# Eighteen instead of nine seven-product tiles in a feed-forward on one Trainium2 core

## The chip, the core and the metric

The kernel runs on one core of a Trainium2 chip. The core has a matrix engine (TensorE, PE in the profile; its weight loads are listed as PEld), a vector engine (VectorE, DVE), an activation engine (ScalarE, ACT), a general engine (GpSimd, POOL) and a queue engine that issues DMAs (SyncE, SP). The time is device microseconds of one execution. Three timed runs of the kernel before gave 1910.76, 1911.52 and 1913.13 us.

## What is computed

Four blocks work on one sequence of 512 tokens with 1024 features, all in float32: a recurrent layer with pooling (`even`), an attention over keys chosen by an index (`odd`), a sliding-window attention with a feed-forward (`swa`, `ffn`), and an attention over compressed, chosen and near keys with a second feed-forward (`nsa`, `ffn`). The parts that the change touches are these:

```python
def rms_norm(x, g):
    y = x32 * lax.rsqrt(jnp.mean(x32 * x32, axis=-1, keepdims=True) + RMS_EPS)
    return y * g
def swiglu(h, w_gu, w_down):                      # D_FF = 2816 = 22 tiles of 128
    gate, up = jnp.split(h @ w_gu, 2, axis=-1)
    return (jax.nn.silu(gate) * up) @ w_down
# second_block, both layers: h = h + swiglu(rms_norm(h, ffn_norm[layer]), ffn_w_gu[layer], ffn_w_down[layer])
# odd_layer: the attention's output is multiplied by silu(z), z a slice of xn @ w_in
```

## The kernel before

Features lie on the 128 partitions and the 512 tokens along the free axis, so the residual is eight tiles X[k] of 128x512. A product keeps float32 accuracy by splitting both factors into a rounded part and a rest (`h` and `l`, type fp32r) and issuing three matmuls: high by high, high by low, low by high (`mm3`, lines 152 to 154). A weight tile is loaded by SP into a `raw` buffer; for each 512 columns ScalarE rounds it into `wh` (line 133) and VectorE or GpSimd takes the rest into `wl` (line 134). The list `wpool["l"]` says which of the two takes the rests of a plain weight. In the feed-forward there are 4 raw buffers and 10 pairs of `wh`, `wl`.

The norm is not multiplied into the matmuls' input: `n.xh`, `n.xl` hold x times the gain, and what a product gives is multiplied by the broadcast reciprocal root `n.RB` afterwards.

In `ffn` a hidden tile j (128 of the 2816 features) needs a gate product and an up product, each with a contraction over 8 feature tiles. A *dense* tile does both plainly: 2 x 8 x 3 = 48 matmuls of 512 columns (`pg`, `pu`). A *scheme* tile (`scheme`, lines 1460 to 1497) treats gate and up as a 2x2 block product over even and odd feature tiles and over the two halves of the tokens, and does it with seven half-size products: 7 x 4 x 3 = 84 matmuls of 256 columns (`pw`). For it, `scheme_weights` forms seven combinations of the raw weights (`s1`, `s2`, differences written back into `raw`), rounds each and takes its rest (lines 1443 and 1444); `token_sums` forms the matching combinations of the tokens once (`ta`, `tb`, split into `th`, `tl`); and eight small operations (lines 1489 to 1496) add the seven products up into `g` and `u`. Before the change, tiles 5, 7, ..., 21 are scheme tiles and the other 13 are dense. Then `g` and `u` give the hidden value: a tanh on ScalarE, two operations on VectorE (1516, 1517) and a split into `hh`, `hl`. The down product (`dn`) is taken over tiles 0 to 7, 8 to 15 and 16 to 21, each time with eight steps of 8 or 6 contraction tiles, between the hidden tiles.

In `ffn` the order on each engine is chosen when the program is built; in `odd` and `nsa` TensorE's order is written by hand: a `Filler` holds a list of projection items, and `f.fill(n)` issues the next n pieces of them between the pieces of the attention. In `odd`, a search for the 256 best keys runs on VectorE (`rounds`: MAX and MATCH_REPLACE, lines 901 and 902) and ends in a `mask` that the attention logits need. A gate projection `zgate` is multiplied by RB (line 826) and turned into silu (lines 1048 and 1049) when its product is done. In `nsa`, `blocks` arranges compressed keys and values into `zp` and splits them (`zh`, `zl`).

Of the kernel before, what the change touches and what calls it, by code (L numbers as in the profile page):

```python
# [31 lines left out]
def kernel(ctx: ExitStack, tc: tile.TileContext, a: dict, out: bass.AP, upto: int = 9, start: int = 1):  # L32
# [783 lines left out]
    def odd(n):  # L816
# [227 lines left out]
        def zgate(m):  # L1044
            def done(ps):
                z = evac(ps)
                t = th[m] = lp.tile([P, T], F32, tag="th", name="th", bufs=6)
                act.activation(t, z, AF.Tanh, scale=0.5)
                dve.scalar_tensor_tensor(t, t, 1.0, z, op0=ALU.add, op1=ALU.mult)
            return proj(5 + m, done)  # L1050

# [19 lines left out]
        with tc.manual_schedule(engines={pe.engine}):  # L1071
# [10 lines left out]
            def k_t(g, j):  # L1082
                return to_feature("kt", kT, g, gqk, j)

            f = Filler([proj(3, index_query), proj(0, latent), proj(1, latent), queries(0), keys(0), zgate(0),
# [5 lines left out]
                        mid(values(3), {2: q_t(3, 0)}), mid(out_part(1, 0), {3: k_t(3, 0), 7: k_t(3, 1)}),  # L1091
                        mid(zgate(6), {1: q_t(3, 1)}), out_part(1, 1), zgate(7),
# [9 lines left out]
            f.fill(9)  # L1102
            index_weights()
            top = topk(1)
# [9 lines left out]
            for i in (2, 3):  # L1114
                for h in range(4):
                    score(i, h)
                    f.fill(1)
                    rounds(1)
            f.fill(3)
            latent_stat()  # L1120
            for i in range(13):
                f.fill(1)
                rounds(1)
                if i == 2:
                    latent_norm()
# [20 lines left out]
            for s in range(len(units) + 3):  # L1146
# [17 lines left out]
                if s >= 3:  # L1164
                    u = s - 3
                    g, j, half, r = units[u]
                    if r == 0:
                        po[g, j, half] = ps_at("po", "po")
                    attend_values(po[g, j, half][:, None, 256 * r:256 * r + 256], half,
# [232 lines left out]
    def ffn(n, layer, gname, goff, after):  # L1402
        es, lp, tmp = open_layer(f"f{layer}", 2, 6, 6, dict(mm=6, at=2))
# [6 lines left out]
        sums = []  # L1410

        def token_sums(q):

            xe, xo, ta, tb = (tmp(nm) for nm in ("xe", "xo", "ta", "tb"))
            for x, k in ((xe, 2 * q), (xo, 2 * q + 1)):
                act.activation(x, X[k], AF.Identity, scale=V("ffn_norm", KD * layer + k))
            t1, t2, t3, t4 = ta[:, :HT], ta[:, HT:], tb[:, :HT], tb[:, HT:]
# [10 lines left out]
        def scheme_weights(j):  # L1428
# [19 lines left out]
            part(a11, dve)  # L1448
# [50 lines left out]
        def hidden(j):  # L1499
            if j >= 5 and j % 2:  # L1500
                g, u = scheme(j)
                pool.tensor_mul(g, g, n.RB)
                dve.tensor_mul(u, u, n.RB)
            else:
                if j == 6:
                    wpool["l"] = [dve, pool]
# [4 lines left out]
                dve.tensor_mul(u, pu, n.RB)  # L1511
            if j < 4:
                token_sums(j)
            th = tmp("th")
            act.activation(th, g, AF.Tanh, scale=0.5)
            dve.scalar_tensor_tensor(th, th, 1.0, g, op0=ALU.add, op1=ALU.mult)
# [635 lines left out]
```

## Time and profile before

| what | value |
|---|---|
| timed runs, median | 1911.52 us |
| profiled execution, its own time | 1910.72 us |
| its span in the trace | 1909.0 us |
| TensorE busy | 1868.6 us (98%), 10334 matmuls |
| VectorE busy | 1360.1 us (71%) |
| ScalarE busy | 1005.0 us (53%) |
| GpSimd busy | 863.8 us (45%) |
| granted TensorE clock, mean | 0.995 |

Matmuls overlap in the pipeline, so a matmul's own duration is longer than its share of the time; what one costs is the distance from its start to the next one's start. Busy time of an engine is read by stage: the two feed-forwards lie at about 900 to 1262 us and 1540 to 1900 us, `odd` at about 480 to 760 us, `nsa` from about 1265 us.

### The profile page before, as it was taken

Reading aid. Unit: us, or ns where it says so; the run is one execution under the profiler, and the core shown is the slowest. Engines: PE = TensorE matmul, PEld = TensorE weight load, DVE = VectorE, ACT = ScalarE, POOL = GpSimd, SP = SyncE. Lnnn points to the kernel's source line nnn. Section 1 sums busy time; section 2 is a strip of 40 time slices with the busy share of each in tenths; the row PEclk is TensorE's granted clock in tenths of the full one; section 3 lists DMA queues with packets and bytes.
Section 4 is the critical chain, followed back from the end, with each engine's and each line's share of the span. In section 5 each row is a group of like instructions: output and inputs, shape, how many; then the busy total and the mean of one; then the engine's idle time right before and its main releaser. Section 6 shows DMA issues by size and latency. Waiting matters only on the chain.

```text
span 1909.0 us, 29335 instructions
## 1 busy us (share of the span) xinstructions
PE 1868.6 (98%) x10334; PEld 1603.1 (84%) x10334; DVE 1360.1 (71%) x2666; ACT 1005.0 (53%) x2079; POOL 863.8 (45%) x842
## 2 busy tenths in 40 slices
PE   8999999999998999999999999999999999999998
PEld 7888888887788888888888898888888888888887
DVE  6776767566698777797786584657999678747553
ACT  6543343434447786696543342347898555324333
POOL 1101001114467575897554453356666455545433
PEclk9999999999999999999999999999999999999999
DMA  4233342322345553411424233333111142423421
GB/s 163 86 109 114 110 144 78 100 78 78 89 127 153 146 158 94 144 45 45 133 89 124 79 107 88 89 131 122 54 45 50 34 144 78 124 76 96 126 75 59
DMA packets 72700, 190.06 MB, mean 100 GB/s; under 512 B 9253, under 2 KB 24101, under 8 KB 72553
## 3 DMA queue, kind: packets, MB, share of 16 engines
q1 hardware_dynamic: 68824, 184.43, 31.8%
q10 hardware_dynamic: 3728, 3.75, 0.6%
q8 instruction: 82, 1.34, 0.3%
q14 instruction: 66, 0.53, 0.1%
HBM read 167.03 MB, written 12.59 MB: 94 GB/s over the span
## 4 chain that ended last, share of the span: by engine, by line
PE 85%; DVE 8%; ACT 2%; DMA 1%; POOL 1%; issue 1%; SPq 0%; DVEq 0%; POOLq 0%; ACTq 0%
PE pj L152 7%; PE pj L153 6%; PE pj L154 6%; PE dn L153 4%; PE dn L152 4%; PE dn L154 4%; PE wo L152 4%; PE wo L154 4%; PE wo L153 4%; PE pw L1484 3%; PE pw L1483 3%; PE pw L1482 3%; PE pu L154 3%; PE pu L153 3%; PE pu L152 3%; PE pg L152 3%
## 5 line engine op out<-in xcount | busy, mean ns | idle before, releaser
L133 ACT CAST wh<-raw 128x512 fp32r<-128x512 f32 (+1 forms) x510 | 306.5, 609 | 396.4 <-PE pj L153 120.8
L134 POOL TENSOR_TENSOR wl<-raw,wh 128x512 fp32r<-128x512 f32 (+1 forms) x226 | 303.5, 1346 | 247.6 <-ACT wh L133 225.1
L134 DVE TENSOR_TENSOR wl<-raw,wh 128x512 fp32r<-128x512 f32 (+1 forms) x284 | 222.1, 788 | 109.8 <-ACT wh L133 103.9
L152 PE MATMUL pj<-xh,wh 128*128 128x512 f32 (+1 forms) x648 | 265.3, 410 | 0.0
L154 PE MATMUL pj<-xh,wl 128*128 128x512 f32 (+1 forms) x648 | 255.4, 394 | 1.0 <-POOL wl L134 0.6
L153 PE MATMUL pj<-xl,wh 128*128 128x512 f32 (+1 forms) x648 | 255.3, 394 | 1.0 <-DVE xl L281 1.0
L154 PEld LDWEIGHTS pj<-xh,wl 128*128 128x128 f32 (+1 forms) x648 | 121.6, 188 | 29.3 <-POOL wl L134 1.0
L153 PEld LDWEIGHTS pj<-xl,wh 128*128 128x128 f32 (+1 forms) x648 | 122.2, 189 | 24.0 <-DVE xl L281 2.1
L153 PE MATMUL dn<-hl,wh 128*128 128x512 f32 (+1 forms) x376 | 141.8, 377 | 0.0
L154 PE MATMUL dn<-hh,wl 128*128 128x512 f32 (+1 forms) x376 | 141.1, 375 | 0.0
L152 PE MATMUL dn<-hh,wh 128*128 128x512 f32 (+1 forms) x376 | 140.7, 377 | 0.0
L152 PEld LDWEIGHTS pj<-xh,wh 128*128 128x128 f32 (+1 forms) x648 | 122.3, 189 | 21.7 <-ACT wh L133 0.9
L152 PE MATMUL wo<-yh,wh 128*128 128x512 f32 x320 | 130.2, 408 | 2.3 <-DVE vv L114 1.4
L153 PE MATMUL wo<-yl,wh 128*128 128x512 f32 x320 | 125.6, 394 | 0.0
L154 PE MATMUL wo<-yh,wl 128*128 128x512 f32 x320 | 125.5, 394 | 0.0
L1444 POOL TENSOR_TENSOR wl<-raw,wh 128x512 fp32r<-128x512 f32 x54 | 76.1, 1410 | 103.5 <-ACT wh L1443 92.4
L744 ACT ACTIVATE L<-L,sm 128x128 f32<-128x128 f32 (+1 forms) x192 | 107.4, 561 | 18.9 <-DVE sm L742 17.8
L742 DVE CUSTOM_DVE_ANT_0 L<-lg,stp 128x128 f32<-128x128 f32 (+1 forms) x192 | 87.6, 482 | 6.3 <-PE lg L796 2.8
L114 DVE TENSOR_TENSOR pl<-pt,ph 128x384 fp32r<-128x384 f32 (+1 forms) x144 | 83.3, 592 | 10.6 <-ACT ph L113 9.3
L1443 ACT CAST wh<-raw 128x512 fp32r<-128x512 f32 x90 | 55.3, 618 | 64.7 <-PE dn L153 33.7
L580 POOL TENSOR_TENSOR up<-u 128x527 f32<-128x527 f32 x8 | 11.1, 1387 | 170.1 <-DVE nq L535 79.5
L323 DVE TENSOR_TENSOR x<-wo,x 128x512 f32<-128x512 f32 x88 | 60.2, 686 | 34.3 <-PE wo L154 33.8
(454 smaller groups left out, 5489.7 us busy)
## 6 DMA issues: line engine op xcount, KB each, us to landing
raw<-in_w_gu SPq DMA_DIRECT2D x88, 512.0 KB, 3.7
raw<-in_w_even SPq DMA_DIRECT2D x48, 512.0 KB, 3.7
raw<-in_w_dn SPq DMA_DIRECT2D x32, 512.0 KB, 3.7
rsc<-rv SPq DMA_DIRECT2D x64, 160.0 KB, 3.8
raw<-in_w_eout SPq DMA_DIRECT2D x16, 512.0 KB, 3.7
stp<-rsc SPq DMA_DIRECT2D x32, 256.0 KB, 3.2
raw<-in_w_odd SPq DMA_DIRECT2D x13, 512.0 KB, 3.8
raw<-in_w_dn SPq DMA_DIRECT2D x16, 384.0 KB, 3.2
```

The lines of the kernel that those rows point to most:

```text
L114: (eng or dve).tensor_sub(l, src, f32(h))
L133: act.copy(h[:, :m], raw[:, o:o + m])
L134: eng[i % len(eng)].tensor_sub(l[:, :m], raw[:, o:o + m], f32(h[:, :m]))
L152: pe.matmul(ps, wh, xh, start=first, stop=False)
L153: pe.matmul(ps, wh, xl, start=False, stop=False)
L154: pe.matmul(ps, wl, xh, start=False, stop=last)
L323: dve.tensor_add(X[k], ps, X[k])
L742: dve.tensor_tensor_reduce(L, lg, strip[:, (1 - ii) * P:], 1.0, -NEG, op0=ALU.add, op1=ALU.min, accum_out=sm[:, ii:ii + 1])
L744: act.activation(L, L, AF.Exp, scale=-1.0, bias=sm[:, ii:ii + 1], accum_out=sm[:, 2 + ii:3 + ii])
L1444: eng.tensor_sub(lv, src, f32(hv))
L1482: pe.matmul(d, h[:, c], xh, start=y == q == 0, stop=False)
L1483: pe.matmul(d, h[:, c], xl, start=False, stop=False)
```

## The change

Tiles 4 to 21 become scheme tiles, 18 of 22. So that they need no multiplication by RB afterwards, the tokens are normed before they are summed: `token_sums` multiplies each x tile by RB on GpSimd, and once the four dense tiles and the down steps over them are issued, `n.xh` and `n.xl` are written anew from the normed tiles. The buffers for that are borrowed from the hidden tiles (12 instead of 11 pairs). The down product is now over tiles 0 to 3, 4 to 9, 10 to 15 and 16 to 21, and the steps of the two middle ones are issued one or two behind each tile from 10 on. In `odd`, `zgate` only copies its product out; norm and silu of it (`silu2`) come when the attention is there. The fills, the index weights and two key transposes of `odd` move by a few pieces. In `nsa` GpSimd takes the weights' rests at first and every second split of `zp`.

```diff
         def zgate(m):
             def done(ps):
-                z = evac(ps)
                 t = th[m] = lp.tile([P, T], F32, tag="th", name="th", bufs=6)
-                act.activation(t, z, AF.Tanh, scale=0.5)
-                dve.scalar_tensor_tensor(t, t, 1.0, z, op0=ALU.add, op1=ALU.mult)
+                with soon():
+                    act.copy(t, ps)
             return proj(5 + m, done)
+        def silu2(m):
+            z, t = th[m], tmp("tz")
+            pool.tensor_mul(z, z, n.RB)
+            act.activation(t, z, AF.Tanh, scale=0.5)
+            dve.scalar_tensor_tensor(z, t, 1.0, z, op0=ALU.add, op1=ALU.mult)
...
-            f = Filler([proj(3, index_query), proj(0, latent), proj(1, latent), queries(0), keys(0), zgate(0),
+            f = Filler([proj(3, index_query), proj(0, latent), proj(1, latent), queries(0), zgate(0), keys(0),
...
-                        mid(values(3), {2: q_t(3, 0)}), mid(out_part(1, 0), {3: k_t(3, 0), 7: k_t(3, 1)}),
-                        mid(zgate(6), {1: q_t(3, 1)}), out_part(1, 1), zgate(7),
+                        mid(values(3), {2: q_t(3, 0)}), mid(out_part(1, 0), {4: k_t(3, 0)}),
+                        mid(zgate(6), {1: q_t(3, 1), 5: k_t(3, 1)}), out_part(1, 1), zgate(7),
...
-            f.fill(9)
+            f.fill(5)
             index_weights()
+            f.fill(4)
...
+            latent_stat()
             f.fill(3)
-            latent_stat()
             for i in range(13):
                 f.fill(1)
                 rounds(1)
-                if i == 2:
+                if i == 1:
                     latent_norm()
...
                         po[g, j, half] = ps_at("po", "po")
+                        if half:
+                            silu2(2 * g + j)
...
     def ffn(n, layer, gname, goff, after):
-        es, lp, tmp = open_layer(f"f{layer}", 2, 6, 6, dict(mm=6, at=2))
+        es, lp, tmp = open_layer(f"f{layer}", 2, 6, 4, dict(mm=6, at=2))
...
         def token_sums(q):
-            xe, xo, ta, tb = (tmp(nm) for nm in ("xe", "xo", "ta", "tb"))
+            xe, xo = (f32(t) for t in hidden_tiles())
+            ta, tb = (f32(t) for t in hidden_tiles())
             for x, k in ((xe, 2 * q), (xo, 2 * q + 1)):
                 act.activation(x, X[k], AF.Identity, scale=V("ffn_norm", KD * layer + k))
+                pool.tensor_mul(x, x, n.RB)
+                normed.append(x)
...
             pool.tensor_add(s1, a21, a22)
-            part(a11, dve)
+            part(a11, pool)
...
         def hidden(j):
-            if j >= 5 and j % 2:
+            if j >= 4:
                 g, u = scheme(j)
-                pool.tensor_mul(g, g, n.RB)
-                dve.tensor_mul(u, u, n.RB)
             else:
-                if j == 6:
-                    wpool["l"] = [dve, pool]
...
-        for j in range(10):
+        for j in range(4):
             hidden(j)
-        down(0, 8, False)
-        for j in range(10, 18):
+        steps = down(0, 4, False)
+        for k in range(KD):
+            run_step(steps)
+            split(n.xh[k], n.xl[k], normed[k])
+        for j in range(4, 22):
+            wpool["l"] = [pool, dve] if j % 2 else [dve, pool]
             hidden(j)
-        down(8, 16, False)
-        for j in range(18, 22):
-            hidden(j)
+            for _ in range(1 + (j % 3 == 0) if j > 9 else 0):
+                run_step(steps)
+            if j in (9, 15):
+                steps = down(j - 5, j + 1, False)
...
-        es, lp, tmp = open_layer("l4", 0, 1, 5, dict(mm=1, at=3, lg=2, po=2), weng=[dve, pool])
+        es, lp, tmp = open_layer("l4", 0, 1, 5, dict(mm=1, at=3, lg=2, po=2), weng=[pool])
...
-                    split(rv[:, :, 0], rv[:, :, 1], zt.rearrange("p (u c) -> p u c", u=4))
+                    split(rv[:, :, 0], rv[:, :, 1], zt.rearrange("p (u c) -> p u c", u=4), pool if t else dve)
...
+            wpool["l"] = [dve, pool]
             f.fill(33)
```

Three places show what moves. The first is VectorE in the first feed-forward, where before a dense tile (`pg`, `pu`) is followed by scheme tile 9 (`pw`; `s_10913` and `s_10914` are its weight sums):

```order
L1510 TENSOR_TENSOR g<-pg,RB 128x512
L134 TENSOR_TENSOR wl<-raw,wh 128x512
L1450 TENSOR_TENSOR s_10914<-s_10913,raw 128x512
L1511 TENSOR_TENSOR u<-pu,RB 128x512
L134 TENSOR_TENSOR wl<-raw,wh 128x512
L1516 SCALAR_TENSOR_TENSOR th<-th,g 128x512
L1517 SCALAR_TENSOR_TENSOR u<-th,u 128x512
L1444 TENSOR_TENSOR wl<-raw,wh 128x512
L1490 TENSOR_TENSOR g<-pw,u 128x256
L114 TENSOR_TENSOR hl<-u,hh 128x512
```

There now one scheme tile follows another; these are the rows from the hidden split of one tile to the second hidden operation of the next:

```order
L114 TENSOR_TENSOR hl<-u,hh 128x512
L1507 TENSOR_TENSOR u<-pw,u 128x256
L1460 TENSOR_TENSOR wl<-raw,wh 128x512
L1508 TENSOR_TENSOR g<-pw,u 128x256
L1509 TENSOR_TENSOR u<-pw,u 128x256
L1510 TENSOR_TENSOR u<-pw,g 128x256
L1511 TENSOR_TENSOR u<-u,pw 128x256
L1512 TENSOR_TENSOR g<-pw,g 128x256
L1460 TENSOR_TENSOR wl<-s_10999,wh 128x512
L1471 TENSOR_TENSOR raw<-raw,s_11000 128x4x128
L1526 SCALAR_TENSOR_TENSOR g<-th,g 128x512
L1460 TENSOR_TENSOR wl<-s_11000,wh 128x512
```

With the second sum of a later tile, the second hidden operation and the first addition, which follow, each tile in this stretch has eight VectorE operations with both inputs in SBUF and seven that read a product from PSUM.

The second place is GpSimd in the same stretch. Before, the weights of a dense tile (line 134) and the multiplication by RB (line 1502) stand between the operations of a scheme tile:

```order
L1447 TENSOR_TENSOR s_10913<-raw 128x512
L134 TENSOR_TENSOR wl<-raw,wh 128x512
L1452 TENSOR_TENSOR raw<-raw 128x4x128
L134 TENSOR_TENSOR wl<-raw,wh 128x512
L1444 TENSOR_TENSOR wl<-raw,wh 128x512 x2
L1502 TENSOR_TENSOR g<-g,RB 128x512
L1444 TENSOR_TENSOR wl<-raw,wh 128x512
```

Now it is one sum, one difference and four rests for every tile:

```order
L1463 TENSOR_TENSOR s_10999<-raw 128x512
L1468 TENSOR_TENSOR raw<-raw 128x4x128
L1460 TENSOR_TENSOR wl<-raw,wh 128x512 x4
L1463 TENSOR_TENSOR s_11143<-raw 128x512
L1468 TENSOR_TENSOR raw<-raw 128x4x128
L1460 TENSOR_TENSOR wl<-raw,wh 128x512 x4
```

These six came once in two tiles before, and come once in every tile.

The third place is VectorE in `odd`, in the search for the best keys. Before, each gate projection puts two operations (lines 826 and 1049) among the rounds:

```order
L901 MAX m_5072<-s_4426 128x8
L826 TENSOR_TENSOR ev<-pj,RB 128x512
L901 MAX m_5075<-s_4426 128x8
L902 MATCH_REPLACE s_4428<-m_5072,s_4426 128x384
L902 MATCH_REPLACE s_4428<-m_5075,s_4426 128x512
L1049 SCALAR_TENSOR_TENSOR th<-th,ev 128x512
L901 MAX m_5081<-s_4428 128x8
```

Now the rounds go on without them:

```order
L901 MAX m_5078<-s_4426 128x8
L114 TENSOR_TENSOR qtl<-tf,qth 128x512
L901 MAX m_5081<-s_4426 128x8
L902 MATCH_REPLACE s_4428<-m_5078,s_4426 128x384
L902 MATCH_REPLACE s_4428<-m_5081,s_4426 128x512
L901 MAX m_5101<-s_4428 128x8
```

What is left between the rounds are splits of transposed queries, keys and values, which were there before too.

## Rows read from the trace of the kernel before

**Rows 1.** Busy time by engine in stretches: stretch, length, PE, PEld, DVE, ACT, POOL, ...
```profile
940.00:960.00 20.00, 20.00 (x89) 16.29 (x88) 18.62 (x22) 11.32 (x19) 14.88 (x13) 1.00 0.16 51
900.00:1262.00 362.00, 362.00 (x1956) 312.79 (x1955) 238.11 (x322) 147.81 (x258) 171.33 (x128) 1.00 0.32 98
1540.00:1890.00 350.00, 350.00 (x1945) 304.81 (x1944) 225.52 (x312) 142.20 (x250) 160.36 (x121) 1.00 0.32 97
```

**Rows 2.** Waits of TensorE in 488 to 600 us: us in total, times, longest.
```profile
PE lg L738 <- DVE mask L907: 2.8, 1, 2.8
PE po L779 <- DVE pl L114: 2.3, 1, 2.3
PE pk L1000 <- POOL ckvl L114: 2.2, 1, 2.2
PE is L883 <- DVE wi L861: 2.0, 1, 2.0
```

**Rows 3.** Waits of TensorE in 600 to 760 us, the longest.
```profile
PE tf L969 <- DVE ktl L978: 1.8, 1, 1.8
```

**Rows 4.** Waits of TensorE in 1262 to 1330 us, the longest.
```profile
PE hp L1678 <- DVE zh L114: 2.2, 1, 2.2
```

**Rows 5.** TensorE in order of time, first matmuls of tiles 4, 5, 6.
```profile
956.08 0.39 PE L152 MATMUL pg<-xh,wh 128*128 128x512 f32 x1
...
967.12 0.28 PE L1482 MATMUL pw<-xh,wh 128*128 128x256 f32 x1
...
977.08 0.40 PE L152 MATMUL pg<-xh,wh 128*128 128x512 f32 x1
```

**Rows 6.** VectorE groups in 967 to 1019 us: count, busy us, mean ns.
```profile
L134 DVE TENSOR_TENSOR wl<-raw,wh 128x512 fp32r<-128x512 f32 x8 | 8.9, 1114 | 0.0
L1516 DVE SCALAR_TENSOR_TENSOR th<-th,g 128x512 f32<-128x512 f32 x5 | 5.4, 1070 | 3.7 <-ACT th L1515 3.7
L114 DVE TENSOR_TENSOR hl<-u,hh 128x512 fp32r<-128x512 f32 x6 | 5.2, 869 | 1.4 <-ACT hh L113 1.4
L1455 DVE TENSOR_TENSOR raw<-raw,s 128x512 f32<-128x512 f32 x2 | 3.6, 1776 | 0.0
L1450 DVE TENSOR_TENSOR s<-s,raw 128x512 f32<-128x512 f32 x2 | 3.5, 1774 | 2.6 <-POOL s L1447 2.6
...
L1491 DVE TENSOR_TENSOR u<-pw,u 128x256 f32<-128x256 f32 x3 | 1.3, 418 | 0.0
```

**Rows 7.** GpSimd groups in 967 to 1019 us.
```profile
L134 POOL TENSOR_TENSOR wl<-raw,wh 128x512 fp32r<-128x512 f32 x8 | 12.4, 1555 | 6.9 <-ACT wh L133 6.9
L1444 POOL TENSOR_TENSOR wl<-raw,wh 128x512 fp32r<-128x512 f32 x6 | 8.6, 1439 | 7.1 <-ACT wh L1443 4.3 <-PE pw L1483 2.5
L1452 POOL TENSOR_TENSOR raw<-raw 128x512 f32<-128x512 f32 x2 | 3.4, 1692 | 0.1
L1502 POOL TENSOR_TENSOR g<-g,RB 128x512 f32<-128x512 f32 x2 | 3.3, 1665 | 5.4 <-DVE g L1496 5.4
L1447 POOL TENSOR_TENSOR s<-raw 128x512 f32<-128x512 f32 x1 | 1.3, 1291 | 5.6 <-PE pw L1483 5.6
```

**Rows 8.** VectorE in order of time: start, us, instruction.
```profile
963.49 0.68 DVE L1517 SCALAR_TENSOR_TENSOR u<-th,u 128x512 f32<-128x512 f32 x1
964.09 0.68 DVE L1510 TENSOR_TENSOR g<-pg,RB 128x512 f32<-128x512 f32 x1
...
968.12 1.78 DVE L114 TENSOR_TENSOR hl<-u,hh 128x512 fp32r<-128x512 f32 x1
```

**Rows 9.** GpSimd in order of time, the same moment.
```profile
967.61 3.45 POOL L134 TENSOR_TENSOR wl<-raw,wh 128x512 fp32r<-128x512 f32 x2
```

**Rows 10.** VectorE groups in 535 to 590 us, the gate projections' two.
```profile
L1049 DVE SCALAR_TENSOR_TENSOR th<-th,ev 128x512 f32<-128x512 f32 x6 | 6.0, 992 | 0.0
L826 DVE TENSOR_TENSOR ev<-pj,RB 128x512 f32<-128x512 f32 x6 | 4.1, 676 | 0.1
```

**Rows 11.** VectorE in order of time ahead of the `zh` split in `nsa`.
```profile
1286.96 1.57 DVE L134 TENSOR_TENSOR wl<-raw,wh 128x512 fp32r<-128x512 f32 x1
...
1293.37 0.67 DVE L134 TENSOR_TENSOR wl<-raw,wh 128x512 fp32r<-128x512 f32 x1
```

More of the change, by code (lines that the diff above doesn't have):

```diff
@@ L1406, in ffn, with hidden_tiles @@
         HT = T // 2
-        sums = []
+        sums, normed = [], []
+        def hidden_tiles():
+            return (lp.tile([P, T], F32R, tag="hh", name="hh", bufs=12),
+                    lp.tile([P, T], F32R, tag="hl", name="hl", bufs=12))
         def token_sums(q):
-            xe, xo, ta, tb = (tmp(nm) for nm in ("xe", "xo", "ta", "tb"))
+            xe, xo = (f32(t) for t in hidden_tiles())
+            ta, tb = (f32(t) for t in hidden_tiles())
             for x, k in ((xe, 2 * q), (xo, 2 * q + 1)):
                 act.activation(x, X[k], AF.Identity, scale=V("ffn_norm", KD * layer + k))
+                pool.tensor_mul(x, x, n.RB)
+                normed.append(x)
             t1, t2, t3, t4 = ta[:, :HT], ta[:, HT:], tb[:, :HT], tb[:, HT:]
@@ L1511, in hidden @@
                 dve.tensor_mul(u, pu, n.RB)
+            th = tmp("th")
+            act.activation(th, g, AF.Tanh, scale=0.5)
+            dve.scalar_tensor_tensor(g, th, 1.0, g, op0=ALU.add, op1=ALU.mult)
+            dve.scalar_tensor_tensor(u, g, 0.5, u, op0=ALU.mult, op1=ALU.mult)
+            h, l = hidden_tiles()
+            split(h, l, u)
+            H.append((h, l))
             if j < 4:
                 token_sums(j)
-            th = tmp("th")
-            act.activation(th, g, AF.Tanh, scale=0.5)
-            dve.scalar_tensor_tensor(th, th, 1.0, g, op0=ALU.add, op1=ALU.mult)
-            dve.scalar_tensor_tensor(u, th, 0.5, u, op0=ALU.mult, op1=ALU.mult)
-            h = lp.tile([P, T], F32R, tag="hh", name="hh", bufs=11)
-            l = lp.tile([P, T], F32R, tag="hl", name="hl", bufs=11)
-            split(h, l, u)
-            H.append((h, l))
         def down(k0, k1, last):
@@ L1534, in down @@
                 run_steps(steps, after)
-            else:
-                for _ in range(KD):
-                    run_step(steps)
+            return steps
         def down_out(k0, k1):
```

## The prediction

> **What bounds the kernel now.** I read the busy time by stretch first. In both feed-forwards TensorE is busy the whole time, 362.00 of 362.00 us and 350.00 of 350.00 us [rows 1], and it waits for nobody there: the list of its waits has no entry in these stretches. So a matmul less is time less there, as long as the engines that feed it keep up. They are not idle: VectorE works 238 of the 362 us, GpSimd 171, and in 940 to 960 us VectorE is busy for 18.62 of 20 us [rows 1]. The reader should keep that row in mind, since it says that in places VectorE is already nearly full. Second, the waits of TensorE outside the feed-forwards: four of 2.0 to 2.8 us around the search for the best keys [rows 2], one of 1.8 us later in the same layer [rows 3], one of 2.2 us at the start of `nsa` [rows 4]. Third, the order of time around one conversion, and the groups of VectorE and GpSimd there.
>
> **What the change takes from TensorE.** Dense tile 4 starts at 956.08, scheme tile 5 at 967.12, tile 6 at 977.08 us [rows 5]: a dense tile costs 11.04 us and a scheme tile 9.96, so each converted tile saves 1.08 us. Nine more tiles in each of two layers are converted: 18 x 1.08 = 19.4 us. The down product has as many matmuls as before (22 contraction tiles, 8 steps), only its split changes. Of this term I am sure if nothing waits.
>
> **What it adds on VectorE and GpSimd.** Here two facts decide. A VectorE operation on two 512-column inputs in SBUF takes 0.68 us, with 0.60 from its start to the next one's (963.49 to 964.09 us), but 1.78 us when GpSimd works beside it [rows 8, 9]; one that reads a product in PSUM keeps its time (0.42 us for 256 columns [rows 6], 0.68 for the one at 964.09 us [rows 8], 0.08 of each overlapping the next). How much is lost on the average comes from the groups of 967 to 1019 us, against 0.68: 8 x 0.43 + 5 x 0.39 + 6 x 0.19 + 2 x 1.10 + 2 x 1.09 = 10.9 us [rows 6], beside 8 + 6 + 2 + 2 + 1 = 19 GpSimd operations [rows 7]: 0.57 us of VectorE for each GpSimd operation.
>
> [...]
>
> In the new stretch, as the order shows, a scheme tile has eight such VectorE operations and seven that read PSUM: 8 x 0.60 + 7 x 0.34 = 7.2 us, and six GpSimd operations of 1.3 us [rows 7]. Before, the same GpSimd work came beside 21 us of matmuls (one dense and one scheme tile); now it comes beside 9.96. VectorE wants SBUF for 4.8 of its 7.2 us, a little more densely than before, so I take 0.70 us lost for each GpSimd operation instead of 0.57: 7.2 + 6 x 0.70 = 11.4 us for a tile, 1.4 more than TensorE needs. Seven such tiles (4 to 10) follow each other without a down step: 7 x 1.4 = 10 us behind. Against that stands the lead. There are ten pairs of weight buffers, a tile uses seven, and tile 4's weights are made while TensorE does the eight down steps over tiles 0 to 3 (8 x 12 matmuls, at 11.04/48 = 0.23 us some 22 us, in which VectorE has only eight additions, eight weight rests and eight rests of the normed tokens to do); the lead is about a tile less one of its seven parts, 8.5 us. So 10 - 8.5 = 1.5 us of waits, and I take 2.5 for each layer, since the queues of both engines are in order and will not be as even as this. The ends: 0, if the loss stays at 0.57 (10.6 us for a tile, 0.7 x 7 = 5 us, within the lead); and 18, if every GpSimd operation costs VectorE the full 1.78 - 0.68 = 1.10 (13.8 us for a tile, 3.8 x 7 - 8.5).
>
> From tile 10 on, down steps of 18 matmuls stand between the tiles, four to three tiles: 3 x 9.96 + 4 x 18 x 0.23 = 46.4 us for TensorE, against 3 x 11.4 + 4 x (0.6 for the addition and about 0.6 for a rest) = 39 on VectorE. Nothing waits there.
>
> The start of the stretch is new as well: eight multiplications by RB on GpSimd (8 x 1.3 = 10.4 us) come ahead of the token sums, eight splits of `xh`, `xl` must follow the last dense tile's reads, and the first down steps need hidden tile 3, which is only just made. TensorE's order puts 34 matmuls over tiles 0 to 2 (7.8 us) ahead of the first over tile 3, and the chain behind that tile's last product is six short steps (multiplication, tanh, two operations, cast, rest: 0.6 to 1.8 us each, 4 to 9 us in all). I take 1.5 us for each layer, between 0 and 4. ScalarE's added casts lie under its 148 of 362 us [rows 1]; the shorter down weights and the same 1 MB of weights per tile find the DMA engines at 0.32 [rows 1].
>
> Sum for the feed-forwards: -19.4 + 2 x (2.5 + 1.5) = -11.4 us.
>
> **`odd`.** Six gate projections no longer put two operations each among the rounds of the search: 6.0 + 4.1 = 10.1 us less on VectorE [rows 10], where it is the engine that the mask waits for. The waits for `mask` (2.8) and for `pl` (2.3), which stand behind these rounds in VectorE's queue, go: -5.1. The wait for `ckvl` (2.2) goes, since the norm of the latent comes one piece earlier and its reader `keys(0)` a whole gate projection later (8 pieces of 3 matmuls, 5.5 us): -2.2. Of the 2.0 for `wi`, the operation moves ahead of the query splits, and TensorE's next product still needs these: one 0.68 us operation less in front, -0.7 (0 to -2.0). The moved key transposes may take the 1.8 us of [rows 3]; I take 0 (0 to -1.8). What is moved out comes back in the attention: eight times a multiplication on GpSimd (1.3), a tanh on ScalarE and one operation on VectorE (0.6 to 1.8), ahead of the last pair of units that needs them; they lie beside TensorE's work, cost 0, and at worst one contended 0.7 us each, 5.6. Together -8.0 (-11 to -2).
>
> **`nsa`.** Two weight rests (1.57 and 0.67 us) stood on VectorE between the broadcast norm and the `zh` split that TensorE waits 2.2 us for [rows 4, 11]. Both go to GpSimd, and half of the splits too: -2.0, between -2.2 and +2 (if a rest on GpSimd, 1.3 against 0.7 us, then comes late for a product).
>
> **Sum.** -11.4 - 8.0 - 2.0 = -21.4 us against the profiled execution, 1910.7 us, which lies 0.8 below the median of the runs; 1889.3, and from the median 1890.1. I say 1889.7.
>
> **Rivals.**
> (1) The two engines' times add up. [...] For it: the 1.78 us. Against it: the loss of 0.57 on the average, with VectorE at 18.62 of 20 us and no wait of TensorE.
> (2) Slower. VectorE becomes the bound of the pure stretch: each GpSimd operation finds it about to start one of its own, loses it 1.10 us, and a tile takes 13.8. Then 18 + 4 us for each layer, 44 in all, and 1910.7 - 29.4 + 44 = 1925. It decides from the point where a tile costs (29.4/2 - 4 + 8.5)/7 = 2.7 us too much, that is a loss of 0.9 us for each GpSimd operation. For it: VectorE loses that much where both run without a gap [rows 8, 9], and now both have work for all of TensorE's time. Against it: seven of fifteen operations don't meet GpSimd.
> (3) `odd` and `nsa` give nothing back: the waits of [rows 2, 4] are followed by others of the same size, since VectorE's search remains the longer chain. 1910.7 - 11.4 = 1899. For it: `odd` has such waits in a row. Against it: 10.1 us leave the chain, twice the waits behind it.
>
> **How the numbers follow.** Forecast 0.58 (1882 to 1896), rival 1 0.20, rival 2 0.08, rival 3 0.14. The range for 8 in 10 takes in the forecast's own, rival 3 and most of rival 1: 1881 to 1906. A measurement of this kernel tells a difference from 0.2%, 3.8 us: below 1907.7 is faster, above 1915.3 slower. Forecast, rival 3 and three quarters of rival 1 are faster, 0.87; the rest of rival 1 and the near side of rival 2 the same, 0.06; slower 0.07.
>
> **What would show it.** In the changed kernel's profile a pair of consecutive scheme tiles should start 10 us apart on TensorE; the list of its waits in the feed-forwards should hold no more than some 4 us in each, by `wl` of VectorE or GpSimd in tiles 7 to 11 and at the first product behind the down steps. VectorE should be busy over 90% in the pure stretch, with a mean of 1.1 to 1.3 us for its rests. In `odd` the waits for `mask` and `ckvl` should be missing. I am wrong in the first place if waits of 10 us and more stand in the pure stretch (rivals 1 and 2), or if scheme tiles that follow each other take another time than 9.96 us.

## The result and the profile after

The changed kernel takes 1934.52 us (median of 4 runs, 1932.68 to 1937.1), the kernel before, on the same chip, 1911.17: a ratio of 1.0126, interval 1.0113 to 1.0138. It is slower by about 23 us; forecast were 21 us less.

The span grows by 23.6 us, from 1909.0 to 1932.6. It falls into four parts, read from the first matmuls of each stage. Up to the first feed-forward 5.2 us are won. The first feed-forward takes 373.3 instead of 360.5 us, `nsa` 279.4 instead of 276.5, and the second feed-forward the rest, some 13 us more. So the loss is in the feed-forwards. Busy time by stretch of the changed kernel (length, PE, PEld, DVE, ACT, POOL, granted clock, DMA share, GB/s), to be held against [rows 1]:

```profile
900.00:1280.00 380.00, 364.69 (x2303) 329.20 (x2302) 309.14 (x400) 166.68 (x311) 255.18 (x180) 0.98 0.33 99
1540.00:1915.00 375.00, 358.61 (x2326) 325.71 (x2325) 306.42 (x396) 167.47 (x313) 253.60 (x174) 0.98 0.31 92
950.00:983.00 33.00, 25.64 (x104) 20.66 (x103) 32.73 (x30) 13.97 (x25) 28.16 (x21) 0.84 0.17 50
983.00:1054.00 71.00, 69.97 (x588) 69.17 (x587) 60.12 (x88) 30.46 (x60) 53.81 (x34) 1.00 0.26 88
```

TensorE has idle time in the feed-forwards now, 15 us in the first stretch, where before it had none. The third line shows where: in 950 to 983 us VectorE is busy for 32.73 of 33 us and GpSimd for 28.16, and TensorE for 25.64 at a granted clock of 0.84. TensorE in order of time, first matmuls of the first down steps, of tile 4, of the first down step behind tile 10, and of tile 11:

```profile
950.84 0.40 PE L152 MATMUL dn<-hh,wh 128*128 128x512 f32 x1
...
982.69 0.28 PE L1498 MATMUL pw<-xh,wh 128*128 128x256 f32 x1
...
1053.96 0.39 PE L152 MATMUL dn<-hh,wh 128*128 128x512 f32 x1
...
1063.51 0.41 PE L1498 MATMUL pw<-xh,wh 128*128 128x256 f32 x1
```

The 96 matmuls over tiles 0 to 3 take 31.85 us instead of the 21.9 that they need when nothing waits (32.93 in the second layer). The seven tiles 4 to 10 take 71.27 us, 1.5 more than 7 x 9.96; the down step behind them takes 9.55 instead of 4.1. Undisturbed tiles do take 9.9 to 10 us, so the saving by conversion is there: it is the waits that outweigh it. The three largest entries in the list of TensorE's waits in 900 to 1280 us (us in total, times, longest):

```profile
PE dn L152 <- ACT hh L113: 11.4, 2, 7.4
PE pw L1498 <- DVE g L1506: 1.3, 2, 0.7
PE pw L1500 <- POOL wl L1460: 1.1, 3, 0.6
```

The cast named as releaser is short (0.62 us, from 965.47); it waited for VectorE (ScalarE idle for 10.75 us ahead of it). What VectorE and GpSimd did while TensorE stood still is seen in their rows (start, us, instruction), first VectorE, then GpSimd:

```profile
953.48 1.79 DVE L114 TENSOR_TENSOR xl<-hh,xh 128x512 fp32r<-128x512 f32 x1
955.19 1.23 DVE L114 TENSOR_TENSOR xl<-hl,xh 128x512 fp32r<-128x512 f32 x1
956.34 1.23 DVE L114 TENSOR_TENSOR xl<-hh,xh 128x512 fp32r<-128x512 f32 x1
957.49 1.79 DVE L114 TENSOR_TENSOR xl<-hl,xh 128x512 fp32r<-128x512 f32 x1
959.20 1.75 DVE L114 TENSOR_TENSOR xl<-hh,xh 128x512 fp32r<-128x512 f32 x1
960.87 1.21 DVE L114 TENSOR_TENSOR xl<-hl,xh 128x512 fp32r<-128x512 f32 x1
962.00 0.68 DVE L1523 TENSOR_TENSOR u<-pu,RB 128x512 f32<-128x512 f32 x1
```

```profile
952.97 1.75 POOL L1468 TENSOR_TENSOR raw<-raw 128x512 f32<-128x512 f32 x1
954.67 1.20 POOL L1434 TENSOR_TENSOR hh<-hh 128x256 f32<-128x256 f32 x1
955.83 1.19 POOL L1435 TENSOR_TENSOR hl<-hl,hh 128x256 f32<-128x256 f32 x1
956.98 1.74 POOL L1460 TENSOR_TENSOR wl<-raw,wh 128x512 fp32r<-128x512 f32 x1
958.68 1.71 POOL L1463 TENSOR_TENSOR s<-raw 128x512 f32<-128x512 f32 x1
960.36 1.17 POOL L1436 TENSOR_TENSOR hh<-hl,hh 128x256 f32<-128x256 f32 x1
```

The two engines go in step: VectorE's starts are 1.71, 1.15, 1.15, 1.71, 1.67 us apart, GpSimd's 1.70, 1.16, 1.15, 1.70, 1.68. In each step both do one operation, the long steps are those with 512 columns on GpSimd, and VectorE's six rests, operations of a size that takes 0.68 us when alone [rows 8], take 1.21 to 1.79 us, as if each waited its turn. The up product of tile 3, done on TensorE at 950.8, is read at 962.00, and TensorE's first matmul over tile 3 starts at 966.14.

### The profile page after: what moved, and what is told of

Read it like the earlier page. It is cut to its first block, busy times and chain, and to the rows that moved or that the text cites. A ratio compares the mean times of both kernels' runs of the same rounds, so it can differ in the third digit from the quotient of the medians.

```text
span 1932.6 us, 31232 instructions
## 1 busy us (share of the span) xinstructions
PE 1863.7 (96%) x10982; PEld 1626.1 (84%) x10982; DVE 1500.9 (78%) x2804; ACT 1043.3 (54%) x2191; POOL 1044.3 (54%) x948
## 4 chain that ended last, share of the span: by engine, by line
PE 65%; DVE 18%; POOL 5%; issue 4%; ACT 4%; DMA 3%; POOLq 0%; SPq 0%; DVEq 0%; ACTq 0%
PE pj L152 6%; PE pj L153 6%; PE pj L154 6%; PE wo L152 3%; PE wo L154 3%; PE wo L153 3%; PE pw L1500 3%; PE dn L153 3%; PE pw L1498 3%; PE pw L1499 3%; PE dn L154 3%; PE dn L152 3%; DMA raw<-in_w_gu 2%; DVE wl L1460 2%; PE po L779 2%
## 5 line engine op out<-in xcount | busy, mean ns | idle before, releaser
L133 ACT CAST wh<-raw 128x512 fp32r<-128x512 f32 (+1 forms) x454 | 262.8, 591 | 250.5 <-PE pj L153 119.6
L134 POOL TENSOR_TENSOR wl<-raw,wh 128x512 fp32r<-128x512 f32 (+1 forms) x196 | 256.4, 1313 | 183.8 <-ACT wh L133 172.0
L134 DVE TENSOR_TENSOR wl<-raw,wh 128x512 fp32r<-128x512 f32 (+2 forms) x258 | 196.0, 766 | 72.9 <-ACT wh L133 67.3
L1460 POOL TENSOR_TENSOR wl<-raw,wh 128x512 fp32r<-128x512 f32 x144 | 226.9, 1598 | 14.6 <-ACT wh L1459 14.6
L152 PE MATMUL dn<-hh,wh 128*128 128x512 f32 (+1 forms) x376 | 143.7, 384 | 23.8 <-ACT hh L113 21.9
L1498 PE MATMUL pw<-th,wh 128*128 128x256 f32 x576 | 162.0, 281 | 1.9 <-DVE g L1506 1.9
L1500 PE MATMUL pw<-th,wl 128*128 128x256 f32 x576 | 162.2, 282 | 0.9 <-POOL wl L1460 0.6
L1499 PE MATMUL pw<-tl,wh 128*128 128x256 f32 x576 | 161.4, 280 | 0.0
L1459 ACT CAST wh<-raw 128x512 fp32r<-128x512 f32 x180 | 105.9, 617 | 66.9 <-DVE raw L1471 40.6
L1500 PE MATMUL pw<-xh,wl 128*128 128x256 f32 x432 | 122.7, 284 | 3.4 <-POOL wl L1460 2.7
L1498 PE MATMUL pw<-xh,wh 128*128 128x256 f32 x432 | 122.2, 283 | 0.0
```

The source lines that it names most:

```text
L133: act.copy(h[:, :m], raw[:, o:o + m])
L134: eng[i % len(eng)].tensor_sub(l[:, :m], raw[:, o:o + m], f32(h[:, :m]))
L152: pe.matmul(ps, wh, xh, start=first, stop=False)
L1459: act.copy(hv, src)
L1460: eng.tensor_sub(lv, src, f32(hv))
L1498: pe.matmul(d, h[:, c], xh, start=y == q == 0, stop=False)
```

## Experiments

Theory A: what counts is the order of VectorE's and GpSimd's queues. Theory B: what counts is the sum of the two engines' times on SBUF, as if they excluded each other there. The pure stretch is tiles 4 to 10, which follow each other without a down step. The sums are GpSimd's weight sums `s1`, one for each converted tile. Times are against the kernel before, 1909.4 to 1910.8 us in the medians beside these runs.

**The rests moved behind tile 3.**
```diff
-            split(n.xh[k], n.xl[k], normed[k])
+            with tc.issue_after(ready.ins):      # ready: rest hl of hidden tile 3
+                split(n.xh[k], n.xl[k], normed[k])
```


> The changed kernel, but VectorE takes the rests xl of the normed inputs behind the rest hl of hidden tile 3 and not ahead of its up product; ScalarE's casts and everything else stay. Theory A (order of VectorE's queue): the six rests that stood ahead of tile 3's up product were what TensorE's first down steps waited for, with the lower clock behind the wait. The first down steps shrink from 31.85 and 32.93 us to 23 to 26 us a layer, the wait of 7.4 us falls under 2, the time is 1915 to 1922 us. Theory B (VectorE and GpSimd together have too little throughput in this stretch, whatever the order): the wait goes to the rests themselves, that is to the first pw products, and the time stays within 5 us of 1934.5.

1933.47 us, ratio 1.0117 (1.0102 to 1.0133): no better. The first down steps took 34.35 us, more than the 31.85. TensorE's waits there:
```profile
PE dn L152 <- DVE x L323: 5.4, 1, 5.4
PE dn L153 <- DVE hl L114: 2.8, 1, 2.8
```
The wait for tile 3 shrank from 7.4 to 2.8 us, as theory A says, but a new one of 5.4 came: the additions `x<-dn` that free the buffers of `dn` now stood behind the same rests. The work has to be done in this stretch, and the order only chooses who waits for it.

**GpSimd's order.**
```diff
-            pool.tensor_sub(a21, a11, a21)
+            with tc.issue_after(rest[-1].ins):   # rest a22 of the tile before, where there is one
+                pool.tensor_sub(a21, a11, a21)
```


> The changed kernel, but on GpSimd the difference a21 (L1468) of a converted tile is taken behind the two rests a21 and a22 of the tile before it, so that their raw buffer comes free, and the next load starts, one operation of 1.8 us earlier; the same instructions otherwise. Theory A (a loop through one raw buffer: sum, difference, two rests, load of about 4.2 us, next sum): the distance of the sums in the pure stretch falls from 11.5 to 11.9 us to 9.9 to 10.4 us, the hidden tiles are in time, the first down step behind tile 10 shrinks from 9.6 to under 6 us, the time is 1923 to 1928 us. Theory B (the two engines exclude each other, so that their common work of 11.5 us a tile is the bound): no operation goes, so the distance stays at 11.5 us and the time within 3 us of 1934.5.

1939.09 us, 1.0146 (1.0128 to 1.0165). Both expectations missed: the sums came 12.3 to 12.5 us apart, not 10, and not 11.5 either. Why it got slower stays open.

**`nsa` as before.**
```diff
-        ... dict(mm=1, at=3, lg=2, po=2), weng=[pool])     # and the z rests and the later list likewise
+        ... dict(mm=1, at=3, lg=2, po=2), weng=[dve, pool])
```


> The changed kernel with the three edits in nsa undone (weight rests by VectorE and GpSimd in turn from the start, the four z rests all on VectorE); the feed-forward and odd edits stay. If these edits themselves cost nsa its 2.9 us more (279.4 instead of 276.5 us), the time is 1930.5 to 1932.5 us and nsa is at 276.5. If nsa is longer because of what the changed feed-forward leaves it at its start, the time stays within 0.8 us of 1934.5.

1933.42 us, 1.0115 (1.0098 to 1.0132), not to be told from the changed kernel; `nsa` took 279.5 us. So the 2.9 us more are not these three edits'. With them undone a wait of 2.1 us for a weight's cast stands in `nsa` that the kernel before does not have. The run with the odd layer's edits alone (below), which has the old feed-forward and the old `nsa`, takes 276.6 us there, so the 2.9 us come with the changed feed-forward ahead of it; by what link stays open.

**Down steps one tile later.**
```diff
-            for _ in range(1 + (j % 3 == 0) if j > 9 else 0):
+            for _ in range({11: 1, 12: 2, 13: 1, 14: 2, 15: 2, 17: 1, ...}.get(j, 0)):
```


> The changed kernel, but the down steps between tiles 10 and 15, and between 16 and 21, begin one tile later (0,1,2,1,2,2 instead of 1,1,2,1,1,2 behind the six tiles). Theory A: the first down step came before hidden tile 9, which runs some 10 us behind and loses 1.6 us more a tile; one tile of delay gives back 3 to 5 us of the 5.5 us a layer, and the steps at tile 16 lose their wait of about 1 us: 1922 to 1930 us. Theory B (VectorE and GpSimd are the bound of the whole stretch): the same lag comes due at the next reader, and the time stays within 3 us of 1934.5 or grows.

1935.54 us, 1.0128 (1.0111 to 1.0145): theory B's number. The first down step took 4.09 us without a wait, but the eight tiles ahead of it took 82.75 instead of 79.7 us and the tile behind it 12.16.

**VectorE's order.**
```diff
-            dve.tensor_sub(s2, s1, a11)
+            with tc.issue_after(done[j - 2].ins), tc.issue_after(last[-1].ins):   # hl two tiles, last rest one tile back (if any)
+                dve.tensor_sub(s2, s1, a11)
```


> The changed kernel, but on VectorE the difference s2 (L1466) of a converted tile is taken behind the hidden rest hl of the tile two before it and behind the last weight rest of the tile before it, so that nothing that frees a raw buffer or makes a hidden tile stands behind a wait for the next load; the same instructions otherwise. Theory A (the in-order queue closes a loop: load of 3.6 us, sum, s2, the up product u, hl, last rest, next load; the trace of the run with the other GpSimd order shows this chain link by link): the distance of the sums in the pure stretch falls from 11.7 to 10 to 10.4 us, the first down step behind tile 10 from 9.6 to under 6 us, and the time is 1922 to 1928 us. Theory B (VectorE's and GpSimd's operations on SBUF exclude each other, and their sum is 11.5 us a tile): the distance stays between 11.3 and 11.9 and the time within 3 us of 1934.5.

1934.84 us, 1.0144 (1.0111 to 1.0178). TensorE, first matmuls as above:
```profile
979.72 0.28 PE L1499 MATMUL pw<-xh,wh 128*128 128x256 f32 x1
...
1056.45 0.39 PE L152 MATMUL dn<-hh,wh 128*128 128x512 f32 x1
...
1060.56 0.28 PE L1499 MATMUL pw<-xh,wh 128*128 128x256 f32 x1
```
This is the plainest case of the five. The down step has lost its wait (4.11 us), and the stretch ahead of it has got it: 76.73 + 4.11 = 80.84 us, where the changed kernel has 71.27 + 9.55 = 80.82. The sums lie 12.6 us apart, which neither theory expected; the time is theory B's. Theory A's loop was real as a chain of waits, but cutting it at this link won nothing. GpSimd's sums still wait for their loads here, 9.4 us in four of them (980 to 1054 us).

**Half of GpSimd's token sums left out** (ScalarE copies into the tiles, so the values are others).
```diff
+                if q < 2:
                     pool.tensor_mul(x, x, n.RB)        # and the four differences likewise
```


> The changed kernel without GpSimd's two products by RB and four differences for the token sums of the last two input pairs (the second half of 24 operations of a layer; ScalarE copies into the two tiles instead, so the converted tiles multiply by wrong values); VectorE's instructions are all there. Theory B (GpSimd's operations hold VectorE up one for one, and that makes the first down steps late): the rests xl fall from 1.2 to 1.8 us to about 0.7 us, the first down steps from 31.85 to under 26 us, the time to 1915 to 1924 us. Theory A (only the order of VectorE's queue counts, and behind it the number of its instructions): the rests stay above 1.1 us and the time above 1929 us.

1922.98 us, 1.0063 (1.0044 to 1.0083), within theory B's range. VectorE's rests in 950 to 970 us (count, busy us, mean ns), in the changed kernel and then in this one:
```profile
L114 DVE TENSOR_TENSOR xl<-hh,xh 128x512 fp32r<-128x512 f32 x3 | 4.8, 1587 | 0.0
L114 DVE TENSOR_TENSOR xl<-hl,xh 128x512 fp32r<-128x512 f32 x3 | 4.2, 1407 | 0.0
```
```profile
L114 DVE TENSOR_TENSOR xl<-hl,xh 128x512 fp32r<-128x512 f32 x4 | 3.8, 956 | 0.3 <-ACT xh L113 0.3
L114 DVE TENSOR_TENSOR xl<-hh,xh 128x512 fp32r<-128x512 f32 x4 | 2.7, 684 | 1.6 <-ACT xh L113 1.6
```
No instruction of VectorE was taken away, and its rests are 0.7 us shorter in the mean (1.50 and 0.82). The first down steps took 27.66 and 25.47 us, the first of them 1.7 more than expected.

**Token sums on VectorE.**
```diff
-                pool.tensor_mul(x, x, n.RB)
+                dve.tensor_mul(x, x, n.RB)             # and the four differences likewise
```


> The changed kernel with the normed products and the four differences of all token sums on VectorE instead of GpSimd (48 operations in the two layers move). Theory B (the two engines exclude each other, so what counts is the sum of their times, and VectorE needs half of GpSimd's time for the same operation): VectorE's rests fall to 0.7 us, the first down steps to 25 to 29 us, the time to 1920 to 1930 us. Theory A (VectorE's own queue is the bound): VectorE gets 6 operations more for each pair, some 12 us a layer, the wait grows, and the time is 1936 to 1955 us.

1923.24 us, 1.0059 (1.0040 to 1.0078): as much as leaving out half of them gave, with 48 operations more on VectorE. Theory A expected 12 us a layer more. This trace has both cases next to each other: GpSimd works until 954.31 us, then not for 14.55 us. VectorE's rests and GpSimd's operations around that moment:
```profile
951.36 1.79 DVE L114 TENSOR_TENSOR xl<-hl,xh 128x512 fp32r<-128x512 f32 x1
953.08 1.78 DVE L114 TENSOR_TENSOR xl<-hh,xh 128x512 fp32r<-128x512 f32 x1
...
955.11 0.68 DVE L114 TENSOR_TENSOR xl<-hl,xh 128x512 fp32r<-128x512 f32 x1
956.65 0.68 DVE L114 TENSOR_TENSOR xl<-hh,xh 128x512 fp32r<-128x512 f32 x1
```
```profile
952.57 1.74 POOL L1468 TENSOR_TENSOR raw<-raw 128x512 f32<-128x512 f32 x1
968.85 6.48 POOL L1460 TENSOR_TENSOR wl<-raw,wh 128x512 fp32r<-128x512 f32 x4 [14.55 <-ACT wh L1459]
```
The same rests on the same engine fall from 1.8 to 0.68 us as soon as GpSimd stops. The first down steps take 27.22 and 25.51 us.

**Tiles 4 to 10 wholly on VectorE as well.**
```diff
+            alt = dve if 4 <= j < 11 else pool
-            pool.tensor_add(s1, a21, a22)
+            alt.tensor_add(s1, a21, a22)               # a21's difference and four rests likewise
```


> The run with the token sums on VectorE, and in converted tiles 4 to 10 also the sum s1, the difference a21 and the four rests of GpSimd on VectorE (six operations a tile move; GpSimd is idle there). Theory B (exclusion: a GpSimd operation holds VectorE up by about 1.1 us, the same operation on VectorE takes 0.6 us): a tile takes VectorE 14 x 0.6 + 7 x 0.34 = 10.8 us instead of 11.5 to 11.9; the stretch of seven tiles with the first down step behind it, 79.6 us in the run with the token sums on VectorE and 80.8 in the changed kernel, falls to 74 to 77 us, the time to 1911 to 1919 us. Theory A (VectorE's own instructions are the bound): six more of 0.6 us a tile lengthen it to some 15 us a tile, the stretch to over 95 us, the time to over 1950 us.

1902.61 us, 0.9962 (0.9951 to 0.9973): 8 us below the lower end expected, and below the kernel before. TensorE's first matmuls, then two stretches:
```profile
948.16 0.40 PE L152 MATMUL dn<-hh,wh 128*128 128x512 f32 x1
...
970.03 0.28 PE L1499 MATMUL pw<-xh,wh 128*128 128x256 f32 x1
...
1046.18 0.39 PE L152 MATMUL dn<-hh,wh 128*128 128x512 f32 x1
```
```profile
950.00:983.00 33.00, 33.00 (x200) 29.49 (x199) 31.88 (x57) 14.84 (x27) 0.00 (x0) 1.00 0.17 53
983.00:1046.00 63.00, 58.10 (x478) 57.59 (x478) 60.09 (x111) 30.37 (x55) 8.68 (x6) 0.97 0.30 95
```
The first down steps now take 21.87 us in either layer: VectorE does 57 operations in the 33 us in which it did 30, in less busy time, because GpSimd does none. That is 9.0 us of what this run gains on the one before it, and the expectation did not count it. The pure stretch did not get shorter: it takes 76.15 us (10.9 a tile, about the 10.8 of VectorE's operations) and its down step 4.11, together 80.26, where 74 to 77 were expected, the run before has 79.60 and the changed kernel 80.82. The rest of the gain lies behind it: from tile 12 on, tiles that took up to 11.7 us are back at 9.9 to 10, but for the last one or two.

**Only the rests of tiles 4 to 10 on VectorE.**
```diff
+            pool.tensor_add(s1, a21, a22)              # and a21's difference; the rests stay with alt
```


> As the run with tiles 4 to 10 wholly on VectorE, but the sum s1 and the difference a21 stay on GpSimd: four rests a tile move. Theory B: two operations of GpSimd remain, beside VectorE's additions from PSUM at best, so a tile takes VectorE 12 x 0.6 + 2.4 = 9.6 us to 11.8 us; the stretch with its first down step takes 73.8 to 79 us, the time is 1908 to 1921 us. Theory A: four more of 0.6 us a tile, the stretch over 90 us, the time over 1940 us.

1905.31 us, 0.9974 (0.9964 to 0.9985); the stretch with its down step some 77 us, shorter than in the run before this, the first down steps longer (23.82), with two GpSimd operations a tile among them. That is in the bounds of theory B, the time 3 us below its range.

**Two dense tiles in the stretch** (GpSimd keeps the weights).
```diff
+            if j in (6, 8):          # pg, pu = dense(...) on n.xh, n.xl; gate and up read from PSUM
```


> The run with the token sums on VectorE, and tiles 6 and 8 of the pure stretch in the plain product on the normed inputs (gate and up read from PSUM without RB): TensorE takes 1.08 us more for each, VectorE and GpSimd have 15 operations fewer. Both theories of the stretch (a tile takes the two engines 11.5 to 11.9 us of which 9.96 are covered) say that the lag of 8 us at the first down step goes: the step shrinks from 9.57 to under 6 us, the pure stretch lengthens by 2.2, the time falls by 3 to 9 us against the run with the token sums on VectorE: 1914 to 1920 us. If the lag has another cause, as the late start of tile 4, the step keeps its wait and the time is 1925 to 1929 us.

1902.96 us, 0.9965 (0.9953 to 0.9977), 11 us below the range. The lag is gone: the step behind tile 10 takes 4.18 us. So are waits of 1 to 2 us in later tiles, which nobody had expected.

**The odd layer's edits alone.** The kernel before, with
```diff
+        def silu2(m):                # zgate copies only; filler, index_weights, latent_stat as in the change
```


> The kernel before with only the odd layer's edits (order of the filler, gate products copied raw and normed later, index weights and latent norm earlier); feed-forward and nsa as before. If what the odd part gave in the changed kernel (its end 5.3 us earlier) is its own, the time is 1904 to 1907 us. If it depends on the feed-forward's weights and buffers around it, or comes back behind it, the time is 1908 to 1911 us.

1904.45 us, 0.9969 (0.9954 to 0.9984). They give 5.9 us of their own.

**Tile 7 dense, and the rest of the stretch on VectorE.**
```diff
+            if j in (7,):            # dense as above; alt = dve if 4 <= j < 11 else pool
```


> The run with tiles 4 to 10 wholly on VectorE, with tile 7 in the plain product on the normed inputs. If the 6.4 us left in the pure stretch are VectorE's operations (10.8 us a tile against 9.96), the dense tile, with some 5 us of VectorE less and 1.08 us of TensorE more, gives back 4 to 5 us of each layer: the stretch with tile 7 takes 70.8 to 73 us, the time is 1892 to 1897 us. If they are not, as with a fixed latency at the start of the converted tiles or the loads, the stretch grows by the 1.08 us and the time is 1903 to 1906 us.

1893.66 us, 0.9912 (0.9898 to 0.9927), the fastest version. TensorE's first matmuls, and the first feed-forward's stretch:
```profile
947.94 0.40 PE L152 MATMUL dn<-hh,wh 128*128 128x512 f32 x1
...
969.81 0.28 PE L1499 MATMUL pw<-xh,wh 128*128 128x256 f32 x1
...
1040.26 0.39 PE L152 MATMUL dn<-hh,wh 128*128 128x512 f32 x1
```
```profile
900.00:1280.00 380.00, 375.68 (x2358) 338.82 (x2356) 310.87 (x472) 174.81 (x326) 171.58 (x141) 1.00 0.35 107
```
Tiles 4 to 10 take 70.45 us, just below the range, and the step behind them 4.10: nothing waits there any more (6 x 9.96 + 11.04 = 70.8). So what was left in the pure stretch was VectorE's operations, and not the loads, which a dense tile needs as well. The feed-forward takes 353.3 us instead of 373.3.

**The sum `s1` back on GpSimd** (tile 7 converted again).
```diff
-            alt.tensor_add(s1, a21, a22)
+            pool.tensor_add(s1, a21, a22)
```


> The run with tiles 4 to 10 wholly on VectorE, with the sum s1 of each tile back on GpSimd. By the count of VectorE's operations alone a tile takes it 13 x 0.6 + 2.4 = 10.2 us instead of 10.8, and the time falls by 6 to 9 us to 1894 to 1897 us. By exclusion the sum holds VectorE up by up to 1.1 us wherever it falls beside an operation on two SBUF tiles (two thirds of VectorE's time), so nothing is won, or up to 4 us lost: 1901 to 1907 us.

1902.27 us, 0.9955 (0.9940 to 0.9971): nothing won. VectorE's busy time in 983 to 1046 us is 60.22 us for 105 operations, and was 60.09 for 111; its rests of the sums (`wl<-s`) take 0.87 us in the mean instead of 0.69 (985 to 1040 us), and its difference `s2` waits 2.8 us in all for the sum. What VectorE saved in operations went into longer ones and this wait; by the count of its operations it should have got 6 to 9 us.

## Why the prediction was wrong

Between the forecast, 21.4 us less, and the trace, 23.6 us more, lie 45 us. In both layers together the start of the stretch cost 21.0 us where 3 were forecast, tiles 4 to 11 cost 14.8 instead of 5, and the tiles behind them 9.5 instead of nothing: 45.3 us in the feed-forwards instead of 8. `nsa` lost 2.9 instead of gaining 2.0, and `odd` gained 5.2 instead of 8.0.

**Conversion, -19.4.** Right: tiles that don't wait take 9.9 to 10 us [rows 5].

**Start of the stretch, +1.5 a layer (0 to 4).** This is the step that failed. It cost 10.0 us in the first layer and 11.1 in the second. The working took "six short steps (...: 0.6 to 1.8 us each, 4 to 9 us in all)" for the chain behind tile 3, as if VectorE were free for it, and took nothing off VectorE for GpSimd's "eight multiplications by RB", though it has 10.4 us of GpSimd for them. Its list of VectorE's work there (additions, weight rests, rests of the normed tokens) also leaves out 11 of the 30 operations of 950 to 983 us: the rests of the token sums, the sums `s2` and a difference, and tile 3's own. The traces show both engines full for 16 us (VectorE busy for 15.99 and GpSimd for 16.02 of the 16.1 us from 950 to 966.1), in step, and the run without half of GpSimd's sums, the one with them on VectorE and the one with GpSimd idle show the price: 31.85 us becomes 27.7, 27.2 and 21.87. Rival 1 added the two engines' times, and priced that for tiles 4 to 10 only; for the start it kept 1.5. That they exclude each other is not shown as such: what the trace has is the equal steps of 1.15 and 1.7 us. 7.4 of the 10 us are the wait for tile 3, and most of the rest is the clock, which no term had: behind the wait TensorE's granted clock is 0.50 over 966 to 971 us, with 0.43 us from matmul to matmul instead of 0.23.

**Tiles 4 to 10, 11.4 us on VectorE and +2.5 a layer (0 to 18).** The sums come 11.5 to 11.9 us apart, so the 11.4 was close, but partly by luck. The working has VectorE at work for all of that time; in 983 to 1054 us it is busy for 60.12 of 71 us, 85% where over 90 were forecast, and GpSimd for 53.81. Neither engine is full. Each turn also holds a wait for a load, since SyncE's loads wait for GpSimd's rests (52.0 us in five waits) and the next sum needs the loaded weights, and VectorE's difference `s2` waits for that sum (waits of GpSimd and of VectorE in this stretch):

```profile
POOL s L1463 <- DMA raw<-in_w_gu: 14.9, 5, 5.7
DVE s L1466 <- POOL s L1463: 8.9, 5, 3.5
```

So the distance here is GpSimd's six operations, lengthened beside VectorE to some 9.8 us, and a load of about 2 us more. How much of it the taking of turns alone makes is not shown: with GpSimd out of these tiles they take as long (80.26 us with their down step, against 80.82), and it needs fewer operations (the dense tiles) to shorten them. The lead of 8.5 us was wrong: TensorE lost 1.5 us in the stretch, 5.45 in the first down step and 1.4 in the tile behind it (this last at a granted clock of 0.50 over 1061.6 to 1066 us), 8.4 in all against 12 us behind (7 x 1.7). In the second layer it lost 6.4. The lead was in the weights, so the products themselves hardly waited; the hidden values had none. TensorE was done with tile 9 at about 1044 (9.96 us ahead of 1053.96). These are that tile's last addition and its hidden value on VectorE; the down step, whose last contraction tile it is, waited for it until 1061.6:

```profile
1053.52 0.42 DVE L1512 TENSOR_TENSOR g<-pw,g 128x256 f32<-128x256 f32 x1
...
1059.27 1.63 DVE L1527 SCALAR_TENSOR_TENSOR u<-g,u 128x512 f32<-128x512 f32 x1
```

**From tile 10 on: "Nothing waits there."** Wrong by 4 us in the first layer and 5.5 in the second: four and five tiles took 10.2 to 11.8 us. With the two dense tiles, and with GpSimd out of tiles 4 to 10, all but the last two or three are back at 9.8 to 10. That they came from the lag carried on is argued from this, not shown link by link.

**`odd`, -8.0 (-11 to -2).** Inside the range: -5.2 by the trace, -5.9 by the run with these edits alone. The waits for `mask` and `ckvl` are gone and that for `pl` is 0.9 [rows 2]; new ones stand behind them:

```profile
PE po L779 <- DVE o L813: 2.1, 1, 2.1
PE is L883 <- ACT rl L885: 1.7, 1, 1.7
```

**`nsa`, -2.0.** Wrong. "Both go to GpSimd" was not so: the two rests stand on VectorE as before, and the wait for `zh` is 2.3 us, where it was 2.2 [rows 4, 11]. The 2.9 us that `nsa` lost are not these edits', as the run with `nsa` as before shows. VectorE ahead of the split:

```profile
1294.48 1.63 DVE L134 TENSOR_TENSOR wl<-raw,wh 128x512 fp32r<-128x512 f32 x1
...
1300.93 0.70 DVE L134 TENSOR_TENSOR wl<-raw,wh 128x512 fp32r<-128x512 f32 x1
```

**Rivals.** Rival 1 gave 1904: it added 8 x 0.60 us of VectorE and 6 x 1.3 of GpSimd to 12.6 us a tile, 2.6 more than TensorE needs, which less the lead of 8.5 makes 10 us of waits a layer, and did not price the same sum at the start. No run shows the 12.6; the sums came 11.5 to 11.9 us apart. Rival 2, 1925, came nearest by luck: its 44 us of waits are close to the 45.3 that the feed-forwards lost, but it had them from 13.8 us for a tile, and a tile took 11.7 in the mean; most of the loss lay at the start and behind tile 11. Rival 3 held for `nsa`, and not for `odd`.

## What to carry to other kernels

Where two engines go in step and both have work all the time, as VectorE and GpSimd did in 953 to 962 us, a stage's price is nearer to the sum of the times that each needs alone than to the longer of them: a step of two operations on 512 columns took 1.7 us, and alone they take 0.68 and 1.3. 32.73 and 28.16 of 33 us in one row are the warning. Where one of them also waits for loads, as in tiles 4 to 10, that sum alone does not give the price. Work that is moved to the slower of two such engines, to relieve the faster, can lengthen both, as it did here with the token sums: VectorE's rests beside them took 1.50 us in the mean, and 0.82 with half of them left out. A lead in one product (weights) is no lead in another (hidden values), so ask of each consumer which of its inputs runs behind. And when a wait is moved by a change of order and the stretch keeps its length, the order was not the bound.

## What the hardware showed

An operation on 512 columns with both inputs in SBUF took GpSimd 1.29 us with VectorE idle for all but 0.07 of them (1306.54 us in the kernel before) and 1.71 to 1.75 in step with VectorE (953 to 962 us in the changed kernel); it took VectorE 0.68 us with GpSimd idle [rows 8] and 1.21 to 1.79 in the same steps. 132 operations with both inputs in SBUF moved to VectorE, 32 of them on 256 columns, made the whole kernel 32 us faster (1934.5 to 1902.6), though VectorE was the engine that was waited for. VectorE's operations on 256 columns with one input in PSUM took 0.41 to 0.43 us in the mean beside GpSimd (983 to 1054 us), and 0.42 in the run with tiles 4 to 10 wholly on VectorE (985 to 1040 us). Behind waits of 7.4 and 4.1 us TensorE's granted clock was 0.50, over 966.1 to 971 and 1061.6 to 1066 us, with 0.43 us from matmul to matmul of 512 columns (968.43 to 968.86) where 0.23 is taken a little later (971.32 to 971.55).
